# Hybrid conformer and neighbourhood-attention block: queries and keys spread over the partition halves with fewer DMA copies, one half written by ScalarE

## The chip, the cores and the metric

The kernel runs on one core of a Trainium2 chip. The metric is the device time of one execution in microseconds, the median of several runs.

## What is computed

One layer on 1024 tokens of 1024 channels, in float32. The input is normalised, projected by one matrix into seven parts, and goes through a convolution branch and an attention branch; both are gated, joined, projected once more, added to the input and normalised. The attention part is the one that the change touches:

```python
hn = rms_norm(h, ln_g[l])
proj = hn @ w_in[l] + b_in[l]
glu_a, glu_b, z_conv, q, k, v, z_att = jnp.split(proj, cuts, axis=-1)
y_conv = conformer_conv(glu_a, glu_b, dw_w[l], dw_b[l], cln_g[l], cln_b[l],
                        pw_w[l], pw_b[l])
y_att = neighbourhood_attention(q, k, v, rpb[l])
...
s = jnp.einsum("bhwd,bhiwjd->bhwij", q_row, k_win).astype(jnp.float32) * scale
```

There are 8 heads of 64 channels. The tokens form a grid of 16 rows by 64 columns, and each token attends to a window of 8 rows by 16 columns around it.

## The kernel before, in words

**Split numbers.** [...] So each operand is held as a high part and a low part, and a full product is made of three matmuls: high by high, high by low, low by high. One projection of 128 channels by 512 tokens is 8 blocks of three such matmuls of 128 x 512 into one PSUM bank: `pq`, `pk` and `pv` for queries, keys and values, `pb`, `pa` and `pz` for the other parts, each for two halves of the tokens (`pk3_0`, `pk3_1`).

**Pairs of heads.** A projection gives 128 channels, two heads: the first in partitions 0 to 63 (`A`), the second in 64 to 127 (`B`). The scores of a head, though, are made with all 128 partitions: the queries hold the head's high part in one half and its low part in the other, and the keys are there twice, once in each half. Per pair `i` there are the tiles `q[0]`, `q[1]`, `kh[0]`, `kh[1]`, `kl[0]`, `kl[1]`, where the index is the head in the pair. A score block is then two matmuls, `q` by `kh` and `q` by `kl` (`scores`, from line 678). Head 2i + a of pair i writes tiles named `s`, the head, the block and the half: `s6_0_0` is the first score block of the first head of the fourth pair.

**How the halves are filled.** `q_out` (line 594) and `k_out` (line 614) take the projection out of PSUM. ScalarE writes the high part for both heads into the tile of the second (`q[1]` or `kh[1]`). VectorE then subtracts it from the same PSUM bank and writes the low part (`ql` or `kl[1]`). What has to go to another half or into the first head's tile is copied by DMAs of 64 partitions by 512 columns, 128 KB each, from SyncE's queue (`copy`, line 591): three per half of `q`, six per half of `k`. Copies that overwrite the place that another copy reads have to wait for that copy.

**What sets the order.** Every engine runs a fixed order. It is made at build time by a planner: generators such as `q_out` and `scores` yield the time at which they can go on, `Clock.weave` picks the next that is due, and each call adds to an assumed clock of its engine. A number after `yield` is thus an assumption on when something lands; it decides where instructions stand, not when they run. `scores` of a pair may be placed once four entries are in `pair[i][4][a]`, two from `q_out` and two from `k_out`. Between the pieces of the attention TensorE does projections; VectorE fills its time with the taps of the depthwise convolution, 31 passes over `acc`; POOL makes the low parts of weights; SyncE's queue also loads weights (`wr`, 512 KB) and bias tables. The queue and each engine work in order: what waits holds up what stands behind it.

**The stretch of a pair.** TensorE does `pq`, `pk` and `pv` for two halves each, and the first scores of the pair come during `pv`. Before them, in the second to fourth pair, stand the transposes `yat` of the pair before, which ScalarE turns into the outputs `ya` by four instructions. In the fourth pair the conv branch's normalisation lies there too: transposes `ln` and `lnb`, rows `xn`.

Of the kernel before, what the change touches and what calls it, by code (L numbers as in the profile page):

```python
# [9 lines left out]
F32 = mybir.dt.float32  # L10
F32R = mybir.dt.float32r
AF = mybir.ActivationFunctionType
# [147 lines left out]
def block(ctx: ExitStack, tc: tile.TileContext, x, xt, vecs, w_in, taps_w, pw_w, pw_b, tab0, tab1, tab2, w_out, final_g, out):  # L160
# [14 lines left out]
    ck = Clock(nc)  # L175
# [11 lines left out]
    def half_tile(tag, name, dt=F32, bufs=1):  # L187
        return att.tile([P, 512], dt, tag=tag, bufs=bufs, name=name)
# [154 lines left out]
    bias = [const.tile([P, NROW * w], F32, name=f"bias{t}") for t, w in enumerate(BW)]  # L343
# [203 lines left out]
    pair = {}  # L547
    A, B = slice(0, 64), slice(64, 128)

    def query(i):  # L550
        for _ in range(2):
            yield from r_u.get()
        q = [U(f"q{i}_{a}", F32R) for a in range(2)]
        pair[i] = [q, None, None, None, [[], []]]
        wq = yield from weight(CH_Q + i)
        bq = qcols[:, i:i + 1]
        for h in range(2):
            pq, sl = yield from proj(wq, h, f"pq{i}_{h}", 16)
            ck.spawn(q_out(i, q, pq, sl, bq), -1)
            if h:  # L560
                r_w.put()
            yield

    def kv(i):
        bk, bv = col(V_BIN + CH_K + i), col(V_BIN + CH_V + i)
        for _ in range(4):
            yield from r_u.get()
        wk = yield from weight(CH_K + i)
        kh = [U(f"kh{i}_{a}", F32R) for a in range(2)]
        kl = [U(f"kl{i}_{a}", F32R) for a in range(2)]  # L570
        pair[i][1:3] = kh, kl
        for h in range(2):
            pk, sl = yield from proj(wk, h, f"pk{i}_{h}")
            ck.spawn(k_out(i, kh, kl, pk, sl, bk), -1)
            if h:
                r_w.put()
            yield
        yield from r_u.get()
        wv = yield from weight(CH_V + i)
        vt = U(f"vt{i}", F32, (P, 8, 2, 64))  # L580
        for h in range(2):
            pvv, sl = yield from proj(wv, h, f"pv{i}_{h}")
            t = ck.act(out=vt[:, :, h, :].rearrange("p g (r c) -> p g r c", c=8),
                       in_=pvv.rearrange("p (r g c) -> p g r c", r=8, c=8), func=AF.Identity, bias=bv)
            r_pj.put(t)
            if h:
                r_w.put()
            yield
        ck.spawn(v_out(i, vt, t), -1)

    def copy(out, in_):
        nc.sync.dma_start(out=out.bitcast(F32), in_=in_.bitcast(F32))

    def q_out(i, q, pq, sl, bq):

        tag, r = (("gz", r_gz), ("ul", r_ul))[sl.start > 0]
        yield from r.get()
        ql = half_tile(tag, f"ql{i}_{sl.start}", F32R, bufs=1 + (tag == "ul"))
        t = ck.act(out=q[1][:, sl], in_=pq, func=AF.Identity, bias=bq)
        yield t  # L600
        t = ck.dve("scalar_tensor_tensor", t, out=ql, in0=pq, scalar=bq, in1=q[1][:, sl].bitcast(F32),
                   op0=ALU.add, op1=ALU.subtract)
        r_pj.put(t)
        copy(q[0][A, sl], q[1][A, sl])
        yield t
        copy(q[0][B, sl], ql[A])
        yield t + 2.8
        pair[i][4][0].append(ck.now)
        copy(q[1][A, sl], ql[B])
        yield ck.now + 2.8  # L610
        pair[i][4][1].append(ck.now)
        r.put()

    def k_out(i, kh, kl, pk, sl, bk):

        t = ck.act(out=kh[1][:, sl], in_=pk, func=AF.Identity, bias=bk)
        yield t
        for half in (B, A):
            copy(kh[0][half, sl], kh[1][A, sl])
        t = ck.dve("scalar_tensor_tensor", t, out=kl[1][:, sl], in0=pk, scalar=bk, in1=kh[1][:, sl].bitcast(F32),  # L620
                   op0=ALU.add, op1=ALU.subtract)
        r_pj.put(t)
        yield t
        for half in (B, A):
            copy(kl[0][half, sl], kl[1][A, sl])
        yield ck.now + 2.8
        copy(kh[1][A, sl], kh[1][B, sl])
        pair[i][4][0].append(ck.now)
        copy(kl[1][A, sl], kl[1][B, sl])
        yield ck.now + 2.8  # L630
        pair[i][4][1].append(ck.now)

    def v_out(i, vt, t):
# [669 lines left out]
```

## Time and profile before

| | |
|---|---|
| median of 3 runs | 552.42 us (551.44 to 553.16) |
| the profiled execution | 554.22 us, span 552.1 us |
| TensorE busy | 527.0 us, 95% of the span |
| VectorE busy | 425.6 us, 77% |
| ScalarE busy | 273.9 us, 50% |
| POOL busy | 169.4 us, 31% |
| mean granted clock of TensorE | 0.991 |
| copies of queries and keys | 72 of 128 KB |

The span is the time from the first to the last instruction in the trace; the execution's own time has what lies around it as well. Busy time is the union of an engine's instructions. TensorE's instructions overlap, so the distance from one start to the next tells what one costs. In the profile's names PE is TensorE, DVE is VectorE, ACT is ScalarE, SP is SyncE (SPq its queue), and PEld is TensorE's load of the stationary operand. The granted clock is a share of 2.4 GHz: 1.00 is that level, 0.50 the lower one of 1.2 GHz.

### The profile page before, as it was taken

What the parts mean: (1) busy time and instruction counts of PE and PEld (TensorE: products, weight loads), DVE (VectorE), ACT (ScalarE), POOL (GpSimd) and SP (SyncE); (2) the same over time, 40 slices, a digit from 0 to 9 for tenths busy, and PEclk for the clock granted to TensorE, in tenths of its full rate; (3) what the DMA queues carried; (4) which work ended last, traced back from release to release, by engine and by line L of the source; (5) the groups of instructions that cost most, each with busy time, mean ns of one, the idle gap of its engine ahead of it and who ended that gap; (6) DMA issues with size and microseconds to landing.
All of it is one profiled execution on the core that took longest, in us unless ns stands there. A gap on an engine that the chain in (4) does not pass through costs nothing. (4 is left out here: it accounts for less than half of the span.)

```text
span 552.1 us, 7499 instructions
## 1 busy us (share of the span) xinstructions
PE 527.0 (95%) x2656; PEld 439.8 (80%) x2656; DVE 425.6 (77%) x709; ACT 273.9 (50%) x656; POOL 169.4 (31%) x142
## 2 busy tenths in 40 slices
PE   5999899999999999999999979999999999999995
PEld 3887687888788888888888768787788788888884
DVE  5439999989899989999999976996764368783232
ACT  6764521246552266534566364567754555462121
POOL 3342204320315400442013442524554354131121
PEclk9999899999999999999999989999999999999998
DMA  8933112542113612344134351110107032034222
GB/s 303 403 115 104 46 38 82 146 118 58 39 60 102 175 58 81 115 112 129 38 108 123 97 143 59 40 58 2 38 1 267 0 116 77 1 138 166 77 77 77
DMA packets 22613, 55.04 MB, mean 100 GB/s; under 512 B 3120, under 2 KB 3248, under 8 KB 22576
## 3 DMA queue, kind: packets, MB, share of 16 engines
q1 hardware_dynamic: 22288, 54.47, 30.8%
q8 instruction: 21, 0.34, 0.3%
q10 hardware_dynamic: 288, 0.09, 0.1%
q14 instruction: 16, 0.13, 0.1%
HBM read 40.92 MB, written 4.19 MB: 82 GB/s over the span
## 5 line engine op out<-in xcount | busy, mean ns | idle before, releaser
L145 DVE SCALAR_TENSOR_TENSOR acc<-glu,dwc,acc 128x512 f32<-128x512 f32 (+25 forms) x150 | 170.5, 1168 | 0.7
L150 POOL TENSOR_TENSOR wl<-wr,wh 128x512 fp32r<-128x512 f32 x48 | 76.1, 1603 | 180.4 <-ACT wh L141 180.4
L130 PE MATMUL pz<-hi,wh 128*128 128x512 f32 x128 | 53.0, 414 | 0.0
L130 PE MATMUL out<-wol,yh 128*128 128x512 f32 (+1 forms) x136 | 51.2, 377 | 0.0
L130 PE MATMUL out<-woh,yl 128*128 128x512 f32 (+1 forms) x136 | 51.2, 376 | 0.0
L130 PE MATMUL out<-woh,yh 128*128 128x512 f32 (+1 forms) x136 | 51.2, 376 | 0.0
L130 PE MATMUL pz<-hi,wl 128*128 128x512 f32 x128 | 50.2, 392 | 0.0
L130 PE MATMUL pz<-lo,wh 128*128 128x512 f32 x128 | 50.1, 391 | 0.0
L141 ACT ACTIVATE pth<-ptp 128x512 fp32r<-128x512 f32 x64 | 32.6, 547 | 18.9 <-PE ptp L136 17.8
L141 ACT ACTIVATE wh<-wr 128x512 fp32r<-128x512 f32 x56 | 32.5, 629 | 17.0 <-PE pq L130 4.8
L141 ACT ACTIVATE prob<-s,mx 128x264 f32<-128x264 f32 (+1 forms) x64 | 33.6, 531 | 14.4 <-DVE mx L145 14.3
L145 DVE TENSOR_TENSOR ptl<-ptp,pth 128x512 fp32r<-128x512 f32 x64 | 38.1, 616 | 0.5 <-ACT pth L141 0.3
L130 PE MATMUL pb<-hi,wh 128*128 128x512 f32 x64 | 27.3, 427 | 7.3 <-ACT wh L141 5.4
L136 PE MATMUL ptp<-ident,prob 128*128 128x128 f32 x224 | 33.5, 273 | 0.5 <-DVE ptl L145 0.5
L145 DVE CUSTOM_DVE_ANT_0 s<-s,bias 128x264 f32<-128x264 f32 (+1 forms) x64 | 30.4, 512 | 2.9 <-PE s L130 2.9
L130 PE MATMUL po<-pth,v 128*128 128x256 f32 x112 | 30.4, 295 | 1.7 <-DVE ytok L145 1.6
L141 ACT ACTIVATE oj<-xr 128x512 f32<-128x512 f32 (+1 forms) x17 | 10.3, 607 | 42.1 <-DVE xr L145 40.9
L130 PE MATMUL po<-ptl,v 128*128 128x256 f32 x112 | 29.2, 287 | 1.3 <-DVE ptl L145 1.3
L145 DVE TENSOR_TENSOR xr<-out,xr 128x512 f32<-128x512 f32 (+1 forms) x17 | 11.2, 658 | 24.9 <-PE out L130 21.8
L141 ACT ACTIVATE os<-po 128x256 f32<-128x256 f32 x32 | 12.3, 386 | 36.3 <-PE po L130 36.2
L130 PEld LDWEIGHTS out<-woh,yh 128*128 128x128 f32 x136 | 25.6, 188 | 4.8
L130 PEld LDWEIGHTS out<-wol,yh 128*128 128x128 f32 x136 | 25.6, 188 | 4.8
(151 smaller groups left out, 1387.6 us busy)
## 6 DMA issues: line engine op xcount, KB each, us to landing
wr<-in_w_in SPq DMA_DIRECT2D x27, 512.0 KB, 3.6
bias<-in_tab SPq DMA_DIRECT2D x16, 276.0 KB, 2.8
xc<-in_xt SPq DMA_DIRECT2D x16, 256.0 KB, 5.6
acc<-in_x SPq DMA_DIRECT2D x8, 512.0 KB, 5.9
wor<-in_w_out SPq DMA_DIRECT2D x8, 512.0 KB, 5.7
xr<-in_x SPq DMA_DIRECT2D x8, 512.0 KB, 3.6
out<-xr SPq DMA_DIRECT2D x16, 256.0 KB, 2.2
kh<-kh SPq DMA_DIRECT2D x24, 128.0 KB, 2.3
```

The source lines that it names most:

```text
L130: self.nc.tensor.matmul(out, lhsT=lhsT, rhs=rhs, start=start, stop=stop)
L136: self.nc.tensor.transpose(out=out, in_=in_, identity=identity)
L141: self.nc.scalar.activation(**k)
L145: getattr(self.nc.vector, fn)(**k)
L150: getattr(self.nc.gpsimd, fn)(**k)
```

## The change

For the queries, ScalarE reads the PSUM bank a second time and writes the first head's half of `q[0]` itself; two copies per half are left, one of each part. For the keys, ScalarE writes the first head's half of `kh[0]` from PSUM in the same way, and after VectorE's low part copies the first head's half of `kl[1]` into `kl[0]`. Four copies per half of the tokens are left, each within a pair of tiles' free halves, and none overwrites what another reads. The assumed landing times change as well: 3.2 after the low part for `q`, 2.0 and 0.6 more for `k`, where it was 2.8 twice.

```diff
         t = ck.act(out=q[1][:, sl], in_=pq, func=AF.Identity, bias=bq)
         yield t
+        ck.act(out=q[0][A, sl], in_=pq[A], func=AF.Identity, bias=bq[A])
         t = ck.dve("scalar_tensor_tensor", t, out=ql, in0=pq, scalar=bq, in1=q[1][:, sl].bitcast(F32),
                    op0=ALU.add, op1=ALU.subtract)
         r_pj.put(t)
-        copy(q[0][A, sl], q[1][A, sl])
         yield t
         copy(q[0][B, sl], ql[A])
-        yield t + 2.8
-        pair[i][4][0].append(ck.now)
         copy(q[1][A, sl], ql[B])
-        yield ck.now + 2.8
-        pair[i][4][1].append(ck.now)
+        yield t + 3.2
+        for a in range(2):
+            pair[i][4][a].append(ck.now)
         r.put()
 
     def k_out(i, kh, kl, pk, sl, bk):
 
         t = ck.act(out=kh[1][:, sl], in_=pk, func=AF.Identity, bias=bk)
         yield t
-        for half in (B, A):
-            copy(kh[0][half, sl], kh[1][A, sl])
+        ck.act(out=kh[0][A, sl], in_=pk[A], func=AF.Identity, bias=bk[A])
         t = ck.dve("scalar_tensor_tensor", t, out=kl[1][:, sl], in0=pk, scalar=bk, in1=kh[1][:, sl].bitcast(F32),
                    op0=ALU.add, op1=ALU.subtract)
         r_pj.put(t)
         yield t
-        for half in (B, A):
-            copy(kl[0][half, sl], kl[1][A, sl])
-        yield ck.now + 2.8
+        copy(kh[0][B, sl], kh[0][A, sl])
         copy(kh[1][A, sl], kh[1][B, sl])
+        t = ck.act(t, out=kl[0][A, sl], in_=kl[1][A, sl].bitcast(F32), func=AF.Copy)
+        yield t
+        copy(kl[1][A, sl], kl[1][B, sl])
+        copy(kl[0][B, sl], kl[0][A, sl])
+        yield max(ck.now, t) + 2.0
         pair[i][4][0].append(ck.now)
-        copy(kl[1][A, sl], kl[1][B, sl])
-        yield ck.now + 2.8
+        yield ck.now + 0.6
         pair[i][4][1].append(ck.now)
```

The planner then orders all engines anew. Three places matter here. Names end in a number of the build, which differs between the two.

SyncE's queue for the keys of the fourth pair, before (`wr26` is a load of weights, the rest are copies, a row with x2 is two of them, into either half):

```order
L592 DMA kh3_0_2930<-kh3_1_2931 64x512 x2
L592 DMA kl3_0_2932<-kl3_1_2933 64x512 x2
L592 DMA kh3_1_2931<-kh3_1_2931 64x512
L592 DMA kl3_1_2933<-kl3_1_2933 64x512
L592 DMA kh3_0_2930<-kh3_1_2931 64x512 x2
L230 DMA wr26_3124<-in_w_in 128x1024
L592 DMA kl3_0_2932<-kl3_1_2933 64x512 x2
L592 DMA kh3_1_2931<-kh3_1_2931 64x512
L592 DMA kl3_1_2933<-kl3_1_2933 64x512
```

and changed:

```order
L592 DMA kh3_0_2902<-kh3_0_2902 64x512
L592 DMA kh3_1_2903<-kh3_1_2903 64x512
L592 DMA kl3_1_2905<-kl3_1_2905 64x512
L592 DMA kl3_0_2904<-kl3_0_2904 64x512
L592 DMA kh3_0_2902<-kh3_0_2902 64x512
L592 DMA kh3_1_2903<-kh3_1_2903 64x512
L230 DMA wr26_3134<-in_w_in 128x1024
L592 DMA kl3_1_2905<-kl3_1_2905 64x512
L592 DMA kl3_0_2904<-kl3_0_2904 64x512
```

Of the second half's copies, the first head's low part (`kl3_0`) was the first behind the load and is now the second and last; the copies of `kh` all stand ahead of the load.

ScalarE at the second half of the keys of the third pair, before:

```order
L141 ACTIVATE po3_3_2240<-ytok1_1802 128x512
L141 ACTIVATE kh2_1_2208<-pk2_1_2271,cols_108 128x512
L141 ACTIVATE ya1_2331<-yat1_0_2332,hcols_139 128x16x16 x2
L141 ACTIVATE ya1_2331<-yat1_1_2340,hcols_139 128x16x16 x2
L141 ACTIVATE wh25_2311<-wr25_2309 128x512 x2
L141 ACTIVATE vt2_2314<-pv2_0_2315,cols_108 128x8x64
```

and changed:

```order
L141 ACTIVATE kl2_0_2183<-kl2_1_2184 64x512
L141 ACTIVATE kh2_1_2182<-pk2_1_2270,cols_108 128x512
L141 ACTIVATE ya1_2325<-yat1_0_2326,hcols_139 128x16x16 x2
L141 ACTIVATE ya1_2325<-yat1_1_2334,hcols_139 128x16x16 x2
L141 ACTIVATE kh2_0_2181<-pk2_1_2270,cols_108 64x512
L141 ACTIVATE kl2_0_2183<-kl2_1_2184 64x512
L141 ACTIVATE wh25_2313<-wr25_2311 128x512 x2
L141 ACTIVATE vt2_2316<-pv2_0_2317,cols_108 128x8x64
```

The second write from the bank (`kh2_0`) and the copy of the low part (`kl2_0`) stand behind the four outputs `ya`.

TensorE at the first scores of the fourth pair, before:

```order
L130 MATMUL pv3_0_3081<-lo7_159,wh23_2969 128x512
L130 MATMUL pv3_0_3081<-hi7_151,wl23_2970 128x512
L130 MATMUL s6_0_0_3156<-kh3_0_2930,q3_0_2652 128x264
L130 MATMUL s6_0_0_3156<-kl3_0_2932,q3_0_2652 128x264
L130 MATMUL s6_0_1_3159<-kh3_0_2930,q3_0_2652 128x288
```

and changed:

```order
L130 MATMUL pv3_0_3095<-hi7_151,wl23_2971 128x512
L130 MATMUL pv3_1_3157<-hi0_144,wh23_2970 128x512
L130 MATMUL pv3_1_3157<-lo0_152,wh23_2970 128x512
L130 MATMUL pv3_1_3157<-hi0_144,wl23_2971 128x512
L130 MATMUL s6_0_0_3162<-kh3_0_2902,q3_0_2652 128x264
L130 MATMUL s6_0_0_3162<-kl3_0_2904,q3_0_2652 128x264
```

The scores moved three projection matmuls to the back; those of the third pair (`s4_0_0`) moved by three as well, those of the second (`s2_0_0`) six to the front, those of the first stand where they stood.

## Rows read from the trace of the kernel before

**Rows 1.** The page: busy time, share of the span and instructions of each engine.

```profile
PE 527.0 (95%) x2656; PEld 439.8 (80%) x2656; DVE 425.6 (77%) x709; ACT 273.9 (50%) x656; POOL 169.4 (31%) x142
```

**Rows 2.** TensorE's waits in the whole span: total us, times, longest us.

```profile
PE s L130 <- DMA kh<-kh: 2.6, 1, 2.6
```

**Rows 3.** Timeline of TensorE, 306 to 331 us: start, duration, what, idle before.

```profile
306.84 0.39 PE L130 MATMUL po<-ptl,v 128*128 128x256 f32 x1 [0.47 <-DVE ptl L145]
...
315.84 0.66 PE L136 MATMUL lnb<-ident,xn 128*128 128x128 f32 x4 [0.87 <-DVE xn L145]
...
320.09 1.09 PE L136 MATMUL yat<-ident,ytok 128*128 128x128 f32 x8 [0.42 <-POOL ytok L150]
...
324.46 0.28 PE L130 MATMUL s<-kh,q 128*128 128x264 f32 x1
327.36 0.56 PE L130 MATMUL s<-kl,q 128*128 128x264 f32 x1 [2.62 <-DMA kh<-kh]
...
330.71 0.39 PE L130 MATMUL pw<-pwh,uh 128*128 128x512 f32 x1
```

**Rows 4.** Busy us by stretches, with granted clock (PEclk), DMA share, GB/s.

```profile
58.00:60.00 2.00, 2.00 (x6) 1.59 (x5) 2.00 (x3) 0.34 (x2) 2.00 (x2) 0.50 0.00 0
...
316.00:320.00 4.00, 3.67 (x20) 2.90 (x19) 3.89 (x6) 3.00 (x7) 3.92 (x3) 1.00 0.60 137
...
328.00:330.00 2.00, 2.00 (x7) 1.63 (x7) 2.00 (x5) 1.51 (x5) 1.50 (x2) 0.50 0.32 69
```

**Rows 5.** Timeline of SyncE's queue, 321 to 324 us.

```profile
321.76 0.34 SPq L230 DMA_DIRECT2D wr<-in_w_in  x1
322.14 1.10 SPq L592 DMA_DIRECT2D kl<-kl  x2
```

**Rows 6.** DMA issues, KB, us to landing: near 322.7, 99 to 104.5, 182.4.

```profile
kl<-kl SPq DMA_DIRECT2D x1, 128.0 KB, 4.6
...
kl<-kl SPq DMA_DIRECT2D x3, 128.0 KB, 2.2
...
kl<-kl SPq DMA_DIRECT2D x1, 128.0 KB, 3.5
```

**Rows 7.** Groups by form, whole span: busy us, mean ns of one, idle before.

```profile
L141 ACT ACTIVATE wh<-wr 128x512 fp32r<-128x512 f32 x56 | 32.5, 629 | 17.0 <-PE pq L130 4.8 <-PE pk L130 4.6 <-DMA wr<-in_w_in 3.4
...
L145 DVE SCALAR_TENSOR_TENSOR kl<-pk,cols,kh 128x512 fp32r<-128x512 f32 x8 | 5.9, 741 | 0.2 <-ACT kh L141 0.2
...
L141 ACT ACTIVATE kh<-pk,cols 128x512 fp32r<-128x512 f32 x8 | 5.5, 683 | 16.0 <-PE pk L130 16.0
```

**Rows 8.** Timelines of ScalarE and VectorE, 117.7 to 118.6 us.

```profile
117.78 0.40 ACT L141 ACTIVATE v<-pvt 128x256 fp32r<-128x256 f32 x1
...
118.49 0.42 DVE L145 TENSOR_TENSOR v<-pvt,v 128x256 fp32r<-128x256 f32 x1 [0.74 <-ACT v L141]
```

**Rows 9.** Timeline of TensorE: the first low-part scores of heads 0 and 2.

```profile
114.59 0.29 PE L130 MATMUL s<-kl,q 128*128 128x264 f32 x1
...
189.33 0.29 PE L130 MATMUL s<-kl,q 128*128 128x264 f32 x1
```

**Rows 10.** Timeline of TensorE at the first scores of head 4.

```profile
253.55 0.39 PE L130 MATMUL pv<-hi,wl 128*128 128x512 f32 x1
253.78 0.28 PE L130 MATMUL s<-kh,q 128*128 128x264 f32 x1
253.90 0.29 PE L130 MATMUL s<-kl,q 128*128 128x264 f32 x1
```

**Rows 11.** Timeline of SyncE's queue: the load in the first pair.

```profile
108.55 0.34 SPq L230 DMA_DIRECT2D wr<-in_w_in  x1
```

**Rows 12.** Timeline of ScalarE: the second pair's keys, second half.

```profile
182.61 0.69 ACT L141 ACTIVATE kh<-pk,cols 128x512 fp32r<-128x512 f32 x1 [4.75 <-PE pk L130]
```

**Rows 13.** Timeline of ScalarE: the outputs in the third pair's stretch.

```profile
250.11 1.57 ACT L141 ACTIVATE ya<-yat,hcols 128x256 f32<-128x256 f32 x4 [1.80 <-DMA kh<-kh]
```

**Rows 14.** Timeline of TensorE near 56 us.

```profile
56.55 0.47 PE L130 MATMUL pb<-hi,wh 128*128 128x512 f32 x1 [1.90 <-DVE sg L145]
```

## The prediction

> **What bounds the kernel now.** The table of busy time comes first: TensorE is at work in 527.0 of 552.1 us [rows 1]. That leaves 25 us, and a change to copies can win only what TensorE idles because of copies, and what its clock loses after such idling. The waits of TensorE, longest first, say how much that is: one wait in the whole span is on a copy, 2.6 us of a score matmul that waits for keys [rows 2]. The timeline of TensorE around it shows the place: head 6, the first head of the fourth pair. The matmul on the high parts starts at 324.46 us, its partner on the low parts only at 327.36 [rows 3]. The table by stretches adds the second price: from 328 to 330 us the granted clock is 0.50, the lower of the two levels [rows 4]. From 327.36 to 330.71 TensorE does three score matmuls and six projection matmuls. At full clock the next start comes 0.12 us after a score matmul and 0.23 after a projection matmul [rows 10], so they would take 3 x 0.12 + 6 x 0.23 = 1.7; they took 3.35. The half clock thus costs 1.6 us and the whole stall 4.2, which is all that the copies cost today. The other three pairs have no wait at this place.
>
> Why this pair is late is read from SyncE's timeline. The load of the next weights is issued at 321.76, the two copies of the low parts right behind it from 322.14 on [rows 5]. A copy in a quiet stretch lands 2.2 us after its issue; the second one behind the load took 4.6; one that went out 1.7 us behind another load took 3.5 [rows 6]. A copy's price thus hangs on whether a 512 KB load stands ahead of it.
>
> **The change part by part.** *Copies removed:* 24 of 72, each 0.55 us of SyncE's time to issue (two take 1.10) [rows 5]. SyncE isn't what the end waits for, so this is worth nothing by itself. With them go the waits of copies on copies that overwrite their source.
>
> *ScalarE work added:* 24 instructions over 64 partitions and 512 columns. No row has this shape. The same columns over 128 partitions take 0.683 us from PSUM and 0.629 from SBUF [rows 7]; at half of that, if time went with elements, 0.34 and 0.31. I take the full rows, since they have the same columns and functions: 16 x 0.683 + 8 x 0.629 = 16.0 us. ScalarE is busy half the span [rows 1], so the sum is hidden; what counts is the latency in the few chains below, where an instruction adds about 0.57, the row less the 0.1 by which neighbours overlap. The Trainium skill, ScalarE: Activation LUTs, section What ACT_TABLE_LOAD costs, lets an activation's time go with its columns alone: 186 ns, 0.833 ns for each, and 93 ns for a bias per partition. By that the 24 would come to an estimated 16 us, and the lower bound falls away; no row here shows it.
>
> *A wait added:* VectorE's low part (`kl`, `ql`) reads the same PSUM bank as ScalarE's second write, and stands behind it in the program. The values' split shows what then happens: ScalarE reads the bank twice from 117.78 on, 0.40 us the first time; VectorE needs only the first result, yet starts at 118.49, some 0.3 after it, when the second is done too [rows 8]. So each of 16 low parts starts some 0.57 later, and VectorE's queue, in order, stands still where its conv taps don't fill the time. The Trainium skill, PSUM — Partial Sum Buffer, section PSUM bank collisions raise a hardware error, says that software keeps two engines off one bank even for reads; the trace agrees. Without such a wait head 4's chain below would end about 0.4 us earlier.
>
> *The score matmuls, pair by pair.* What the first head's low part needs is now: ScalarE's second write, VectorE's low part (0.74 us [rows 7]), a ScalarE copy (0.57), two issues (0.55 each, the urgent one last), a landing.
> - Head 0: needed at 114.59 [rows 9]. The load goes out at 108.55 [rows 11]; all four copies are behind it now, the urgent one issued at about 110.4, and by 3.5 to 4.6 it lands at 113.9 to 115.0. Stall 0 to 0.4, I take 0.1.
> - Head 2: the scores stand six projection matmuls earlier, 189.33 - 1.38 = 187.95 [rows 9]. High part at 182.61 [rows 12], second write until 183.85, low part 184.6, copy 185.2, second issue from 185.75. The load of this pair goes out between its two halves, some 4 us earlier, so the landing is nearer to 2.2 than to 3.5: 187.95, at most 189.25. Stall 0 to 1.3, I take 0.2.
> - Head 4: needed at 253.90 + 0.69 = 254.6, three projection matmuls later [rows 10]. The second write stands behind the four attention outputs `ya`, 1.57 us from 250.11 on [rows 13], whose transposes move up by three projection matmuls. `ya` then runs from 249.4 to 251.0, the second write until 251.55, low part 252.3, copy 252.85, second issue from 253.4, landing 255.6 by 2.2. Stall 1.0; 0 if half the partitions cost half and `ya`, which in its row waits 1.80 for copies, starts earlier; 2.3 if the copy gets behind a load and lands in 3.5.
> - Head 6: the conv tiles' transposes move up in TensorE's order, so of the three small waits ahead [rows 3] I expect those of 0.47 and 0.42 to go and 0.87 to stay: -0.9. Needed at 324.46 - 0.9 + 0.69 + 0.12 = 324.4. The copy stands behind `ya` again: transposes at 320.09 - 0.9 = 319.2, `ya` from half a microsecond later until 321.3, copy 321.9, second issue from 322.45. The load, 0.9 earlier as well, is 1.6 ahead of it, so by 3.5 it lands at 325.9. Stall 1.5 instead of 2.6: -1.1. By 2.2 the stall would be 0.2, by 4.6 it would be 2.6.
>
> *The clock.* The idle time of 0.87 at 315 us left the clock at 1.00, one of 1.90 near 55 us was followed by 0.50 [rows 3, 4, 14]. At 1.5 I take it that the clock stays up: -1.6. *After head 6* the order is nearly that of before, and I count nothing.
>
> **Sum:** -1.1 - 0.9 - 1.6 + 0.1 + 0.2 + 1.0 = -2.3 us. The profiled execution took 554.22 us, span 552.1 plus 2.1 around it, 1.8 above the median; it would come to 551.9, and the median of 552.42 to **550.1**.
>
> **The rivals.**
> 1. *The stall of head 6 is shorter, yet the clock falls all the same.* For it: 1.5 is nearer to 1.90 than to 0.87. Then -1.6 is gone: -0.7, 551.7. A change that is hidden altogether gives the same reading. It lies within 0.3% (1.7 us), about what a measurement of this kernel can tell from no change.
> 2. *Slower: the second write is queued too deep.* ScalarE's queue puts it behind `ya` (heads 4 and 6) or the conv's normalised rows (head 6), and VectorE, then the copy, wait for it in order. It decides from the point where head 4 stalls for as long as 1.9, which brings the half clock there too. Then head 4 costs 2.0 + 1.6, heads 0 and 2 0.3 + 0.4, head 6 stalls as before: +4.3 - 0.9 = +3.4, 555.8; without the half clock +1.8, 554.2. For it: the places in ScalarE's order, and the load ahead of the urgent copy in pairs one and four. Against it: every link is a fraction of a microsecond, and in three of four pairs no copy is late today.
> 3. *All copies come in time,* since fewer share the queue and none waits for another. Then -2.6 - 0.9 - 1.6 = -5.1, 547.3. Against it: the load still goes out ahead of the last two copies in pair four.
>
> **How the numbers follow.** Forecast 0.40, of which 0.05 falls within 0.3%; rival 1 0.30; rival 2 0.20; rival 3 0.10. Faster 0.45, same 0.35, slower 0.20. The range goes from rival 3, 547.3, to rival 2 without the half clock, 554.3, which leaves out rival 2's dearer half and what no case covers. The forecast's own range is 548.4 to 551.3: the landing at head 6 between 2.6 and 4.2, and head 4 between 0.2 and 1.5.
>
> **What would show it.** In the profile of the changed kernel the waits of TensorE should name a score matmul in head 6 with 1 to 2 us and head 4 with about 1; the low parts of VectorE should start after ScalarE's second write; the granted clock around the scores of head 6 should be 1.00. A stall at head 4 above 1.9 and a clock of 0.50 near 256 us would make rival 2 right; no wait on copies at all rival 3. The prediction is wrong in its ground if TensorE's waits move to the conv part after 340 us, which I took as unchanged, or if VectorE idles for several microseconds in all for ScalarE between 80 and 320 us and the taps come late.

## The result, and the profile after

The changed kernel is slower: 556.12 us median of 18 runs against 552.48 of before. The medians lie 3.6 us apart; the ratio over all of the runs is 1.0053 with a 95% interval of 1.0037 to 1.0069, which is 2.9 us. The forecast was 550.1, with 554.3 as the upper end of its range. The profiled execution has a span of 554.5 us, 2.4 more than that of before.

The page of the changed kernel, busy time of each engine (compare [rows 1]):

```profile
PE 527.8 (95%) x2656; PEld 440.1 (79%) x2656; DVE 425.8 (77%) x709; ACT 287.4 (52%) x680; POOL 168.0 (30%) x142
```

ScalarE's 24 new instructions are there, 13.5 us more busy time, and TensorE's busy time is all but the same. So the loss is idle time of TensorE and clock. These are the longest of TensorE's waits in the whole span that differ from before (total us, times, longest):

```profile
PE s L130 <- ACT wh L141: 3.2, 1, 3.2
PE lnb L136 <- DVE xn L145: 2.1, 2, 1.3
...
PE s L130 <- issue: 1.5, 2, 1.2
PE ln L136 <- DVE ptl L145: 1.4, 1, 1.4
```

Where before had one wait of a score matmul for keys, 2.6 us [rows 2], there are three now: 3.2, 1.2 and 0.3. The timeline of TensorE gives their places (start, duration, what, idle before and its releaser):

```profile
187.88 0.36 PE L130 MATMUL s<-kl,q 128*128 128x264 f32 x1 [0.26 <-issue]
...
255.60 0.36 PE L130 MATMUL s<-kl,q 128*128 128x264 f32 x1 [1.20 <-issue]
...
308.83 1.07 PE L136 MATMUL ln<-ident,acc 128*128 128x128 f32 x8 [1.45 <-DVE ptl L145]
...
316.93 0.66 PE L136 MATMUL lnb<-ident,xn 128*128 128x128 f32 x4 [1.28 <-DVE xn L145]
...
327.00 0.28 PE L130 MATMUL s<-kh,q 128*128 128x264 f32 x1
330.51 0.56 PE L130 MATMUL s<-kl,q 128*128 128x264 f32 x1 [3.23 <-ACT wh L141]
```

These three waits are all at low parts (`s<-kl`), of heads 2, 4 and 6. The name `wh` behind the last is only the event that came last; what the matmul needed was a copy, and SyncE's queue shows it:

```profile
322.35 2.99 SPq L592 DMA_DIRECT2D kh<-kh  x2
325.44 0.53 SPq L230 DMA_DIRECT2D wr<-in_w_in  x1
326.02 1.10 SPq L592 DMA_DIRECT2D kl<-kl  x2
```

Two copies of `kh` take 2.99 us from the first's start, where two that are ready take 1.10. The second writes the half of `kh[1]` that VectorE's low part reads, so it waits for that instruction, and the load of weights behind it waits with it. The load goes out at 325.44, not at 321.76 as in [rows 5], 0.58 us ahead of the two copies of the low parts. The list of DMA issues from 325 to 330.6 us (KB each, median us to landing) tells what they then took, beside the last copy ahead of the load:

```profile
wr<-in_w_in SPq DMA_DIRECT2D x1, 512.0 KB, 4.1
kl<-kl SPq DMA_DIRECT2D x2, 128.0 KB, 4.0
kh<-kh SPq DMA_DIRECT2D x1, 128.0 KB, 2.2
```

The urgent copy is the second of the two, issued at about 326.5, and lands 4 us later, when the matmul starts. The table by stretches shows the clock after it (PEclk, the figure behind POOL's; the rows at 330 to 336 are the lower level):

```profile
328.00:330.00 2.00, 0.00 (x0) 0.00 (x0) 1.97 (x4) 0.33 (x1) 0.00 (x0) 0.82 0.58 189
330.00:332.00 2.00, 1.49 (x5) 1.42 (x6) 1.60 (x5) 1.17 (x3) 1.62 (x2) 0.50 0.00 0
332.00:334.00 2.00, 2.00 (x6) 1.52 (x6) 0.12 (x2) 1.26 (x5) 1.08 (x1) 0.50 0.40 102
334.00:336.00 2.00, 2.00 (x6) 1.56 (x5) 0.00 (x0) 0.00 (x0) 0.00 (x0) 0.50 0.84 224
```

From 330.51 to 336.04 TensorE starts three score and eleven projection matmuls; at full clock they take 3 x 0.12 + 11 x 0.23 = 2.9 us, here 5.5. The half clock costs 2.6, against 1.6 before.

Put together for the two profiled executions: waits on copies 4.7 instead of 2.6, +2.1; half clock +1.0; the small waits between 300 and 322 us 2.7 instead of 1.8, +1.0. One start-up wait of before (1.3 us, VectorE's low part at the first projection) is not in this trace and another of 0.3 is, -1.0: it lies ahead of the change. That makes +3.1, where 2.4 was seen; of the other 0.7, 0.4 is one small wait after 340 us that is gone, and the rest I didn't trace. Both traces also have a stretch at the lower clock near 58 us, behind the wait of 1.9 us of [rows 14]; it costs both alike and isn't in this difference.

### The profile page after: what moved, and what is told of

It is laid out like the page before. It is cut to its first block, busy times and chain, and to the rows that moved or that the text cites. A ratio compares the mean times of both kernels' runs of the same rounds, so it can differ in the third digit from the quotient of the medians.

```text
span 554.5 us, 7486 instructions
## 1 busy us (share of the span) xinstructions
PE 527.8 (95%) x2656; PEld 440.1 (79%) x2656; DVE 425.8 (77%) x709; ACT 287.4 (52%) x680; POOL 168.0 (30%) x142
## 5 line engine op out<-in xcount | busy, mean ns | idle before, releaser
L150 POOL TENSOR_TENSOR wl<-wr,wh 128x512 fp32r<-128x512 f32 x48 | 73.4, 1548 | 182.9 <-ACT wh L141 182.9
L130 PEld LDWEIGHTS out<-woh,yl 128*128 128x128 f32 x136 | 25.6, 188 | 4.7
```

Source lines behind the costliest of these rows:

```text
L130: self.nc.tensor.matmul(out, lhsT=lhsT, rhs=rhs, start=start, stop=stop)
L150: getattr(self.nc.gpsimd, fn)(**k)
```

## The experiments

The theory after this result (A): the time is lost in the chain of the keys' copies, above all at head 6, where a copy that waits holds back a load, which then lands on the urgent copy. The rivals: the planner's new order costs it (B), or ScalarE's added work and VectorE's wait for it (C). Where a text below says that an engine's order stays, it is the same row for row.

### The plan and the operations apart

The operations of the change, with the planner given the costs of before: ScalarE's added calls are issued without being counted, and the yields are those of before. In part, against the changed kernel:

```diff
-        ck.act(out=kh[0][A, sl], in_=pk[A], func=AF.Identity, bias=bk[A])
+        nc.scalar.activation(out=kh[0][A, sl], in_=pk[A], func=AF.Identity, bias=bk[A])
...
-        yield max(ck.now, t) + 2.0
+        yield ck.now + 2.8
```

> The changed kernel's operations and copies, but the planner is given the costs and landing times of the kernel before, so TensorE's and VectorE's orders are word for word those of before. Theory A (the copies' chain costs the time: the low keys' copy is later, and the load held behind a waiting copy goes out right ahead of it): slower than before, by a stall at head 6 that is as long as before's 2.6 us or longer, about 3.2, with a longer half clock; 553 to 555.5 us, ratio 1.001 to 1.005; the waits of 1.45 (transposes of the conv) are back at 0.5. Theory B (the new plan costs the time, the operations nothing): the time of before, ratio 0.998 to 1.002, and a stall at head 6 of 2.6 or less.

Measured: 1.0094 (1.0058 to 1.013), slower as theory A has it, but by twice what it foresaw. And the reverse, the operations of before with dummy costs that stand for the change's, in part, against the kernel before:

```diff
+        ck.queue("act", 0.07 + 0.00084 * 512 + 0.09, None)
         t = ck.dve("scalar_tensor_tensor", t, out=kl[1][:, sl], in0=pk, ...
...
-        yield ck.now + 2.8
+        t = ck.queue("act", 0.07 + 0.00084 * 512, t)
+        yield t
+        yield max(ck.now, t) + 2.0
```

> The other half: the copies of the kernel before and no new ScalarE instruction, but the planner counts the changed kernel's costs and landing times, so TensorE's and VectorE's orders are those of the changed kernel. Theory A: the low part's copy of head 4 is in time (no 1.2 us wait) and head 6 stalls about 2.6 as before; only the conv's waits (1.45 and 1.28 us, together 1.0 more than before's three) stay; ratio 1.000 to 1.003. Theory B: as slow as the changed kernel, ratio 1.004 to 1.007.

Measured: 0.9935 (0.9911 to 0.9959), which neither theory expected. So there are four corners:

| ratio to before | operations of before | operations of the change |
|---|---|---|
| plan of before | 1 | 1.0094 |
| plan of the change | 0.9935 | 1.0053 |

The new plan is worth 3.6 us by itself, and the new operations cost 5 to 7 us in either plan. Theory B falls. Why the plan gains is in SyncE's queue and TensorE's timeline of that kernel at head 6:

```profile
322.79 1.10 SPq L592 DMA_DIRECT2D kl<-kl  x2
323.93 0.58 SPq L230 DMA_DIRECT2D wr<-in_w_in  x1
```

```profile
325.88 0.36 PE L130 MATMUL s<-kl,q 128*128 128x264 f32 x1 [0.69 <-DMA kl<-kl]
```

The load stands behind the two copies here, and the wait is 0.69. In the changed kernel the copies of the low parts are issued only once ScalarE's copy is planned to be done, and in that gap the planner put the load.

### Queries or keys

The change's plan, with the key part of before and the query part of the change (first), and the other way round (second):

> The changed kernel's plan, its query part too, but the keys' copies and writes are those of the kernel before. The two plan runs gave 0.9935 for the new plan with the old operations and 1.0094 for the old plan with the new ones. Theory A (the keys' chain costs the time): as with all the old operations, 547.5 to 549.5 us, ratio 0.992 to 0.996, head 6 stalls under 1 us and the clock stays up. Theory C (ScalarE's second writes and VectorE's wait for them, of queries and keys alike): half the gain, ratio 0.997 to 1.001.

Measured: 0.9962 (0.9942 to 0.9983), between the ranges of the two theories and nearer to A's.

> The complement: the changed kernel's plan and its key part, the queries' copies and writes of the kernel before. Theory A: as slow as the changed kernel, ratio 1.003 to 1.006, stalls of about 1.2 at head 4 and 3 at head 6. Theory C: half of the loss, ratio 0.997 to 1.001.

Measured: 1.0053 (1.0032 to 1.0074), the changed kernel's own ratio, with waits of 1.27 at head 4 and 3.27 at head 6. So the keys carry the loss. The query part costs nothing that these runs can tell: beside the keys' part it adds nothing (1.0053 with it and without), and alone it has 0.9962 against 0.9935, with intervals that overlap.

### The order on SyncE alone

```diff
         copy(kh[0][B, sl], kh[0][A, sl])
-        copy(kh[1][A, sl], kh[1][B, sl])
         t = ck.act(t, out=kl[0][A, sl], in_=kl[1][A, sl].bitcast(F32), func=AF.Copy)
         yield t
-        copy(kl[1][A, sl], kl[1][B, sl])
         copy(kl[0][B, sl], kl[0][A, sl])
+        copy(kh[1][A, sl], kh[1][B, sl])
+        copy(kl[1][A, sl], kl[1][B, sl])
```

> The changed kernel with one edit: the second copy of the high keys, which waits for VectorE's low part, and the second copy of the low keys go out behind the one that the first head's low part needs. All orders but SyncE's stay. Theory A: the load at head 6 is no longer held behind that copy and goes out near 323 instead of 325.4, the urgent copy is issued at about 325.5 and lands by 2.2 to 3 us at 327.7 to 328.5; head 6 stalls 0.5 to 1.5 instead of 3.2 without a half clock, head 4 0.6 instead of 1.2; 549.5 to 552 us, ratio 0.995 to 0.999. Theory B, and a theory C by which ScalarE's added work and VectorE's wait for it cost the time: no gain, ratio 1.004 to 1.007.

Measured: 1.0006 (0.9987 to 1.0024), which lies between the ranges of the theories; the waits are as theory A has them. SyncE's queue and TensorE's timeline at head 6:

```profile
321.21 0.46 SPq L592 DMA_DIRECT2D kh<-kh  x1
321.90 0.40 SPq L230 DMA_DIRECT2D wr<-in_w_in  x1
324.38 0.46 SPq L592 DMA_DIRECT2D kl<-kl  x1
```

```profile
326.69 0.36 PE L130 MATMUL s<-kl,q 128*128 128x264 f32 x1 [0.56 <-ACT wh L141]
...
330.22 0.50 PE L130 MATMUL pw<-pwh,ul 128*128 128x512 f32 x1 [1.75 <-DVE ul L145]
```

The load goes out 3.5 us earlier, the urgent copy 2.5 us behind it, and lands in 2.2 us. The wait falls from 3.23 to 0.56, the clock stays at 1.00 there. Part of the gain is given back: VectorE's `ul` is late next, 1.75. The edit has two halves, which were run apart. First, only `kh[1]`'s copy goes to the end:

> The changed kernel with half of the edit of the run that put the urgent copy first (1.0006): only the high keys' second copy, which waits for VectorE's low part, moves behind the low keys' copies; those keep their order, the urgent one second. Theory A1 (the harm is the load that this copy holds back on SyncE until it lands on the urgent copies): the load goes out near 322 again, the urgent copy at about 325, head 6 waits 1.0 to 1.7; most of the gain is there, ratio 0.999 to 1.003. Theory A2 (the harm is that the urgent copy is the second of two, 0.55 us): ratio 1.003 to 1.006, head 6 waits 2.7 or more.

Measured: 1.0024 (1.0007 to 1.0042). The load goes out at 322.61 and head 6 waits 1.20:

```profile
322.61 0.41 SPq L230 DMA_DIRECT2D wr<-in_w_in  x1
325.09 1.10 SPq L592 DMA_DIRECT2D kl<-kl  x2
```

```profile
328.05 0.36 PE L130 MATMUL s<-kl,q 128*128 128x264 f32 x1 [1.20 <-ACT wh L141]
```

Then, only the two copies of `kl` change places:

> The other half of that edit: the urgent copy goes out ahead of its partner, the high keys' second copy still stands ahead of the load and waits. Theory A1: the load still goes out within a microsecond ahead of the urgent copy, head 6 waits 2.3 to 3 us and the clock halves; ratio 1.002 to 1.005. Theory A2: ratio 0.999 to 1.002.

Measured: 1.004 (1.0021 to 1.0059). Head 6 still waits 3.08, and the load is again 0.57 us ahead of the copies:

```profile
319.50 2.97 SPq L592 DMA_DIRECT2D kh<-kh  x2
322.58 0.52 SPq L230 DMA_DIRECT2D wr<-in_w_in  x1
323.15 1.10 SPq L592 DMA_DIRECT2D kl<-kl  x2
```

By the waits at head 6, the held load (3.23 to 1.20) is the larger part, and theory A1 holds; being second costs about half a microsecond more, once the load is out of the way. The ratios of the two lie too near to each other to tell them apart.

### The same thing in the kernel before

If the load's place is what counts, the kernel before must gain by it too. One line moved: its two copies of the low keys are put on the queue ahead of the `yield` at which the load slipped in; all other orders stay.

```diff
         r_pj.put(t)
-        yield t
         for half in (B, A):
             copy(kl[0][half, sl], kl[1][A, sl])
+        yield t
```

> The kernel before, with one line moved: the two copies of the low keys stand on SyncE's queue ahead of the load where the planner put the load in between (in the first pair and the fourth); all other orders are those of before. If the gain of the new plan is that the load comes after these copies (theory A), this gives it to the old plan as well: the copies of head 6 go out at 321.3 right after the low part and land by 2.2 to 3 us at 323.5 to 325, head 6 waits under 0.6 instead of 2.6 and the clock stays at 1.00; 2.6 and 1.6 less, ratio 0.992 to 0.996. If the gain comes from the other moves of the plan, the ratio stays at 0.998 to 1.002.

Measured: 0.9937 (0.9916 to 0.9959). SyncE's queue, TensorE's timeline and the clock at head 6:

```profile
320.23 1.10 SPq L592 DMA_DIRECT2D kl<-kl  x2
321.37 0.58 SPq L230 DMA_DIRECT2D wr<-in_w_in  x1
```

```profile
323.53 0.29 PE L130 MATMUL s<-kl,q 128*128 128x264 f32 x1
```

```profile
328.00:330.00 2.00, 2.00 (x14) 1.89 (x13) 1.78 (x3) 1.54 (x5) 1.35 (x2) 1.00 0.24 90
```

No wait and no half clock: the 4.2 us that the prediction read from [rows 3, 4] as the price of that stall come back nearly whole, 3.5 us.

### ScalarE's part in it

The second write, of queries and keys alike, reads the first one's result in SBUF instead of the bank; all orders stay. The keys' part of the edit:

```diff
-        ck.act(out=kh[0][A, sl], in_=pk[A], func=AF.Identity, bias=bk[A])
+        nc.scalar.activation(out=kh[0][A, sl], in_=kh[1][A, sl].bitcast(F32), func=AF.Copy)
+        ck.queue("act", 0.07 + 0.00084 * 512 + 0.09, None)
```

> The changed kernel with one edit: ScalarE's second write reads the first one's result in SBUF instead of the PSUM bank, so VectorE's low part shares the bank with no later reader and needs only the first write. All orders stay. Theory C (VectorE's wait for the second write, 3.7 us of idle between 60 and 345 us, costs the time): those idles go, ratio 0.998 to 1.002. Theory A: at head 6 the low part stands behind taps, not behind ScalarE, so its stall stays at about 3; head 4 is up to 0.5 better; ratio 1.003 to 1.006.

Measured: 1.004 (1.002 to 1.006). VectorE's waits from 60 to 345 us, the changed kernel's and then this one's:

```profile
DVE kl L145 <- ACT kh L141: 2.2, 3, 0.8
...
DVE ql L145 <- ACT q L141: 1.5, 3, 1.0
```

```profile
DVE ql L145 <- ACT q L141: 0.4, 1, 0.4
...
DVE kl L145 <- ACT kh L141: 0.2, 1, 0.2
```

The idles shrink from 3.7 to 0.6 us, as foreseen (the kernel before has 0.8), and the wait of `lnb` near 317 us is gone; but head 6 waits 3.73, and the time isn't told apart from the changed kernel's. Theory C is out as the main cause. The Trainium skill, PSUM — Partial Sum Buffer, section PSUM bank collisions raise a hardware error, tells software to keep two engines off one bank; that VectorE waits for a second reader of its bank, and no longer does when that reads SBUF, agrees with it.

Then ScalarE's copy was taken out of the chain: the other half is copied straight from VectorE's result, and ScalarE writes the first head's own half beside that transfer. Against the changed kernel:

```diff
         copy(kh[0][B, sl], kh[0][A, sl])
-        copy(kh[1][A, sl], kh[1][B, sl])
+        copy(kl[0][B, sl], kl[1][A, sl])
         t = ck.act(t, out=kl[0][A, sl], in_=kl[1][A, sl].bitcast(F32), func=AF.Copy)
         yield t
+        copy(kh[1][A, sl], kh[1][B, sl])
         copy(kl[1][A, sl], kl[1][B, sl])
-        copy(kl[0][B, sl], kl[0][A, sl])
```

> The changed kernel with one edit more than the run that put the urgent copy first: the other half's low keys are copied straight from VectorE's result, as before, and ScalarE's copy of the own half runs beside that transfer instead of ahead of it. Orders of all engines but SyncE stay. Theory A: the urgent copy goes out 0.6 to 0.8 us earlier than there (323.7 instead of 324.4), but at head 6 VectorE's low part comes late itself; heads 4 and 6 wait 0 to 0.4 instead of 0.6 each; ratio 0.996 to 1.000, against 1.0006. If it stays at 1.0006, the chain through ScalarE's copy isn't what is left, but SyncE's order alone was.

Measured: 0.9958 (0.9941 to 0.9976); no score matmul waits for a copy, and the load is behind the urgent copy again (324.88 after 324.31). With the second writes from SBUF as well:

> The same with ScalarE's second writes read from SBUF, so that VectorE's low part has no second reader of its PSUM bank ahead of it. Theory A: VectorE's idles of 3.7 us in all go, its taps and low parts come up to 1 us earlier by head 6, the waits of the conv's transposes there shrink from 1.45 and 1.28; ratio 0.992 to 0.997, the new plan's gain with nothing taken back. If VectorE's wait for the bank costs nothing, the time of the run beside it.

Measured: 0.9931 (0.9907 to 0.9955). That is the new plan's whole gain, with the change's fewer copies in it, and it beats both kernels. From 0.9958 it isn't clearly told apart, since the intervals overlap. Of the two waits of the conv's transposes only that of 1.28 is gone; the other is 1.58.

Last, the two ways together: the plan of before, the copy ahead of the load, and the fewer copies mended as above.

> A version meant to beat both kernels: the plan of the kernel before with the low keys' copy on SyncE ahead of the load (that alone gave 0.9937), and in it the changed kernel's fewer copies, mended: ScalarE writes the first head's own half from SBUF, the other halves are copied straight from the full results, so no ScalarE instruction stands in a chain and VectorE has no later reader of its bank. Theory A (copies cost time only by their place against the load and the waits ahead of them; their number is worth nothing): the same as without the fewer copies, ratio 0.992 to 0.996, no copy wait of TensorE over 0.5 us. If 24 fewer copies are worth something by themselves: 0.991 or lower. If ScalarE's 24 instructions cost something by themselves: 0.997 or more.

Measured: 0.9946 (0.9929 to 0.9963), no better than the one moved line alone (0.9937). 24 copies fewer and the 24 ScalarE instructions in their place come to nothing that can be measured; these runs don't show either of the two alone.

## Why the prediction was wrong

- **What bounds the kernel: right.** Only the stall at head 6 was to be won, and the one-line run won it.
- **Head 6, the step that failed:** "The load, 0.9 earlier as well, is 1.6 ahead of it, so by 3.5 it lands at 325.9." The rows of SyncE's order ahead of the prediction show the load behind both copies of `kh`, but I didn't ask what the second of them waits for. It waits for VectorE's low part, which reads the half that it overwrites, so the load came 3.7 us later than before instead of 0.9 earlier, and only 0.58 ahead of the copies. The landing was 4, not 3.5, and the stall 3.23, not 1.5: -1.1 became +0.6.
- **The low part itself, in the same step:** I took ScalarE's `ya` as the last link ahead of ScalarE's copy. Here it wasn't; the copy waited 0.67 us for VectorE, whose order now has five taps and a row of the conv ahead of the low part, where before it had two taps. The timelines, before and then changed:

```profile
318.39 2.19 DVE L145 SCALAR_TENSOR_TENSOR acc<-glu,dwc,acc 128x512 f32<-128x512 f32 x2
320.51 0.74 DVE L145 SCALAR_TENSOR_TENSOR kl<-pk,cols,kh 128x512 fp32r<-128x512 f32 x1
```

```profile
318.13 5.46 DVE L145 SCALAR_TENSOR_TENSOR acc<-glu,dwc,acc 128x512 f32<-128x512 f32 x5
323.51 0.68 DVE L145 SCALAR_TENSOR_TENSOR xn<-th,xn 128x512 f32<-128x512 f32 x1
324.11 0.74 DVE L145 SCALAR_TENSOR_TENSOR kl<-pk,cols,kh 128x512 fp32r<-128x512 f32 x1
324.88 0.63 ACT L141 ACTIVATE kl<-kl 64x512 fp32r<-64x512 f32 x1 [0.67 <-DVE kl L145]
```

Even so, with the load out of the way the wait was 1.20; the held load made it 3.23.

- **The clock:** "I take it that the clock stays up: -1.6" hung on a stall of 1.5. With 3.23 it fell for longer: +1.0. At head 4's 1.20 it stayed up, as assumed.
- **Small waits:** -0.9 became about +1.0. Those of 0.47 and 0.42 went as foreseen. But the transposes `ln`, moved up, now wait 1.45 for VectorE (1.4 with the plan alone, so that is the plan's), and the 0.87 grew to 1.28, by VectorE's wait for the bank (with the second write from SBUF that wait is gone).
- **Right in size:** head 0 none (0.1 foreseen), head 2 0.26 (0.2), head 4 1.20 (1.0). At head 4 the chain is the one foreseen: the second write stands behind `ya`, the low part waits for that write, and the copy for the low part.

```profile
249.09 1.57 ACT L141 ACTIVATE ya<-yat,hcols 128x256 f32<-128x256 f32 x4 [1.12 <-PE yat L136]
250.53 0.68 ACT L141 ACTIVATE kh<-pk,cols 64x512 fp32r<-64x512 f32 x1
251.25 0.75 DVE L145 SCALAR_TENSOR_TENSOR kl<-pk,cols,kh 128x512 fp32r<-128x512 f32 x1 [0.83 <-ACT kh L141]
252.03 0.64 ACT L141 ACTIVATE kl<-kl 64x512 fp32r<-64x512 f32 x1 [0.82 <-DVE kl L145]
```

- **Also right:** the 64-partition writes took 0.673 us from PSUM and 0.631 from SBUF, the whole of the 128-partition rows, as I chose, not half. By the rule of the Trainium skill, ScalarE: Activation LUTs, section What ACT_TABLE_LOAD costs, an estimate of 0.71 and 0.61 comes out; the trace agrees to 0.04 us.
- **A sign of being wrong that came:** between 80 and 320 us VectorE idled 3.7 us for ScalarE's writes, as the prediction had feared, but with those idles gone the ratio was still 1.004.
- **The rivals:** rival 2, with a chance of 0.20, gave 555.8, near to what was measured, but that is luck in the number. Of its links, `ya` in ScalarE's queue delayed head 4, by 1.2 us where the forecast had 1.0; the half clock at head 4 didn't come, and head 6 was held mainly by the load. Its sum without the half clock is 554.2, so the range's end of 554.3 is 0.1 too high. That the plan itself could gain was not among the cases: a plan that set the load behind the copies is worth 3.6 us, and the operations took it back.

Not settled: why the change's operations cost more under the old plan (1.0094) than the waits at heads 4 and 6 there (1.0 and 3.1) and the conv's add up to. Its trace, of the slowest of its six executions, shows that the loss isn't at these places alone: TensorE already trails the kernel before by 0.7 us at 219 us (0.5 of it from the start) and by 2.3 at 250, ahead of head 4, and by 6.1 at 334. VectorE's waits for ScalarE's high parts of queries and keys, from 60 to 345 us, are 6.8 us there, against 0.8 before and 3.7 in the changed kernel:

```profile
DVE ql L145 <- ACT q L601: 3.6, 5, 1.6
DVE kl L145 <- ACT kh L618: 3.2, 3, 1.3
```

So under that plan ScalarE's second writes may cost more; no run takes these waits alone away there.

## What to carry to other kernels

Before you reckon with when a transfer goes out, read its queue row by row, and ask of each row ahead of it what it waits for: one copy that waits for another engine moves everything behind it. A small urgent transfer belongs ahead of a large load that isn't urgent; here that took one moved line and was worth 0.6%, while a third fewer copies, with ScalarE's work in their place, came to nothing. And when a planner orders the work, run the new costs with the old operations and the reverse: the sum of the two can hide that one gains and the other loses.

## What the runs showed of the hardware

A 128 KB copy from SBUF to SBUF took 2.2 us from issue to landing alone. Behind a load of 512 KB, in seven of the traces between 60 and 345 us, it took 3.6 to 4.6 us when issued within 1 us of the load and 2.2 to 3.0 us when issued 2.5 us or more behind it; in between both occur. The clock at full level outlived idle times of 1.20, 1.45 and 1.75 us and fell after those of 3.08 to 3.73 and, in the kernel before, after 2.62. The wait of 1.89 or 1.90 us near 56 us [rows 14] is in all fourteen traces: in seven the clock fell to 0.50 after it, in seven it stayed at 1.00. So the length of one idle time alone doesn't decide it, and a price of the clock that is read from one trace needn't be paid in each execution. The times show it too: over the 18 runs of the changed kernel the mean granted clock was between 0.988 and 0.996, and the time went with it, 556.25 to 557.76 us in the nine at 0.988, 552.17 to 553.87 in the four at 0.996.
